# FFN projections of a macaron decoder trunk: three 256-column matmuls per weight tile in place of a 512- and a 256-column one, at other start addresses

## The chip, the cores and the metric

The kernel runs on one core of a Trainium2 chip. The metric is device time of one execution in microseconds (us); lower is better. Engines are named as the profile names them: PE is the tensor engine's matmul, PEld its weight load, DVE the vector engine, ACT the scalar engine, POOL GpSimd, SP the engine that issues most DMAs.

## What is computed

The reference is a decoder trunk with two layers on a sequence of 256 positions, D_MODEL = 1024, D_FF = 2816, all in float32. Cut to what matters:

```python
for layer in range(DEPTH):
    x = x + 0.5 * swiglu_ffn(rms_norm(x, ffn1_norm[layer]), ffn1_w_gate_up[layer], ffn1_w_down[layer])
    h = rms_norm(x, mix_norm[layer])
    x = x + (conv_mixers(h, ...) if layer % 2 == 0 else dilated_attention(h, ...))
    x = x + 0.5 * swiglu_ffn(rms_norm(x, ffn2_norm[layer]), ffn2_w_gate_up[layer], ffn2_w_down[layer])
return rms_norm(x, final_norm)

def swiglu_ffn(x, w_gate_up, w_down):
    gate, up = jnp.split(x @ w_gate_up, 2, axis=-1)
    return (jax.nn.silu(gate) * up) @ w_down
```

So there are four FFNs, with a convolution mixer after the first and attention after the third.

## The kernel before

**Layout.** Activations lie transposed: `x` is 8 blocks of 128 channels by 256 positions. All weights come as one stream of 162 units of 16 tiles (128 x 128 each, 1 MB a unit), loaded on SP into `raw`.

**Products from split operands.** Float32 accuracy comes from splitting each operand into a part rounded to fp32r and its remainder. `split` (L118) turns a unit into `w1` (ACT copy, L127) and `w2` (DVE subtraction, L128); `split_to` (L184) does the same for activations, so that `xs[:, k, 0]` and `xs[:, k, 1]` (and `gs[:, f, 0]`, `gs[:, f, 1]`) are the two parts of a block, each of 256 columns, one behind the other. A product is w1·b0 + w1·b1 + w2·b0. It is written in two ways. `mm3` (L159) makes three matmuls of 256 columns into one sum (L163, L164, L165). `mm2` (L167) makes one matmul of 512 columns, w1 with both parts side by side (L169), and one of 256 columns, w2 with the first part (L170); this leaves two sums, that have to be added later. Each matmul has its own weight load. Columns that are streamed are 768 per weight tile in both.

**An FFN** (`ffn`, L365) has 22 gate/up units p, each with 16 weight tiles: 8 contraction blocks for the gate, then 8 for the up part. Most units use `project2` (L325), with a PSUM bank each for gate and up, and then `join` (L335): an ACT copy of one half of the bank (L339), a DVE addition (L340), and a multiplication by the norm's factor (L341). The first four units of the first FFN, the first two of the fourth, and the last of each (`ONES`, `ONE_END`) use `project` (L315) with `mm3`, and only the multiplication (L382). In the first FFN the first unit comes from a separate bank, computed ahead. Then follow silu, product and split into `gs` (L386 to L389). The down projection runs over 8 output blocks d of 22 tiles each; the first seven use `mm2` and two additions into `x` (L405), the last `mm3` and one. After each block, `after.add(d)` prepares the next stage's `xs` block.

**Order.** `advance` (L131) issues loads and splits a fixed number of units ahead of use. PE runs in program order. At an FFN's start the sum of squares of `x` goes through two matmuls of 256 columns (L252, L253, in `rsqrt_wide`), which are placed among the first units' matmuls.

**Start addresses.** `xs` lies in one buffer that begins at a multiple of 1024 bytes (`LINE`, `BASE`), and each norm places its `xs` at `XS_START` bytes in it: 288 or 32 for the FFNs, 192 for conv (layer 0), 256 for attention. Blocks are 2048 bytes, so every part has its start at the same place modulo 1024. `gs` is placed by `GS_START`.

**The conv mixer** uses `project`, so `mm3`, for eight of its ten column pairs, with `xs` at 192; the pairs 2 and 9 are plain float32 (L161). Attention's query and key projections use `project2` for 8 units.

Of the kernel before, what the change touches and what calls it, by code (L numbers as in the profile page):

```python
# [10 lines left out]
F32 = mybir.dt.float32  # L11
# [3 lines left out]
ALU = mybir.AluOpType  # L15
PSUM = bass.MemoryType.PSUM

P = 128
D = 1024
S = 256  # L20
DEPTH = 2
FF = 2816
ND = D // P
NF = FF // P
# [9 lines left out]
UT = 16  # L34
# [14 lines left out]
FINE = {13: 4, 14: 4, 6: 4}  # L49
PRIO_C = 500  # L50
PRIO_R = 500
ONES = [4, 0, 0, 2]
ONE_END = 1
PRIO_F = 0
FFN_STEP = 40
QK2 = 1
# [3 lines left out]
WIDEC = 0  # L60
LINE = 1024
BASE = 16512
XS_START = {"F1": (288, 32), "MX": (192, 256), "F2": (288, 32)}
GS_START = (800, 800, 800, 736)
GROUPS = ((0, 2), (2, 4), (4, 6), (6, 8))
M_POOL = [0, 0, 0, 0]
T_POOL = [0, 0, 0, 0]
# [27 lines left out]
def trunk(ctx: ExitStack, tc: tile.TileContext, xin, wst, cst, bia, idn, out):  # L95
    nc = tc.nc
# [7 lines left out]
    psb = ctx.enter_context(tc.tile_pool(name="psb", bufs=4, space=PSUM))  # L104
# [26 lines left out]
    def advance(u, ahead_split=ahead_split):  # L131
        while at["load"] < min(n_units, u + ahead_load):
            load(at["load"])
            at["load"] += 1
        while at["split"] < min(n_units, u + ahead_split):
            split(at["split"])
            at["split"] += 1
# [16 lines left out]
    def take(n):  # L154
        st = Stream(used[0])
        used[0] += n
        return st

    def mm3(o, a, b, start, stop, check=False):  # L159
        if len(a) == 1:  # L160
            nc.tensor.matmul(o, a[0], b[-1], start=start, stop=stop, skip_group_check=check)  # L161
            return
        nc.tensor.matmul(o, a[0], b[0], start=start, stop=False, skip_group_check=check)  # L163
        nc.tensor.matmul(o, a[0], b[1], start=False, stop=False, skip_group_check=check)  # L164
        nc.tensor.matmul(o, a[1], b[0], start=False, stop=stop, skip_group_check=check)  # L165

    def mm2(o, w, b, start, stop):  # L167

        nc.tensor.matmul(o, w[0], b, start=start, stop=False, skip_group_check=True)  # L169
        nc.tensor.matmul(o[:, 0], w[1], b[:, 0], start=False, stop=stop, skip_group_check=True)  # L170


    x = keep.tile([P, ND, S], F32, name="x")
# [10 lines left out]
    def split_to(o1, o2, src, scale=None):  # L184

        if scale is None:
            nc.scalar.copy(o1, src)
            nc.vector.tensor_sub(o2, src, o1.bitcast(F32))
        else:
            nc.scalar.activation(o1, src, AF.Copy, scale=scale)  # L190
            nc.vector.scalar_tensor_tensor(o2, src, scale, o1.bitcast(F32),  # L191
                                           op0=ALU.mult, op1=ALU.subtract)
# [119 lines left out]
    def twice(r):  # L312
        return r[:, None, :].to_broadcast([P, 2, S])

    def project(st, base, xs, xg=None):  # L315

        bank = psa.tile([P, 2, S], F32, name="pa")
        for i in range(2):
            for k in range(ND):
                w = st.tile(base + 2 * k + i)  # L320
                b = (xs[:, k, 0], xs[:, k, 1]) if len(w) == 2 else (xg[:, k],)
                mm3(bank[:, i], w, b, k == 0, k == ND - 1)
        return bank

    def project2(st, base, xs):  # L325

        banks = []
        for i in range(2):
            bank = psa.tile([P, 2, S], F32, name="pa")
            for k in range(ND):  # L330
                mm2(bank, st.tile(base + 2 * k + i), xs[:, k], k == 0, k == ND - 1)
            banks.append(bank)
        return banks

    def join(v, banks, r):  # L335

        for i, bank in enumerate(banks):
            h = tmp.tile([P, S], F32, name="sq")
            nc.scalar.copy(h, bank[:, 1])  # L339
            nc.vector.tensor_add(v[:, i], bank[:, 0], h)  # L340
        nc.vector.tensor_mul(v, v, twice(r))  # L341

    def ffn_first(norm, after):

        with tc.tile_pool(name="sp", bufs=1, reuse_waits="tile") as sp:
            xg = sp.tile([P, ND, S], F32, name="xg0")
            bank = psa.tile([P, 2, S], F32, name="pa")
            for k in range(ND):
                nc.vector.tensor_scalar_mul(xg[:, k], x[:, k],
                                            const[:, norm.col + k:norm.col + k + 1])  # L350
                for i in range(2):
                    c = slice((2 * k + i) * P, (2 * k + i + 1) * P)
                    nc.tensor.matmul(bank[:, i], raw[0][:, c], xg[:, k],
                                     start=k == 0 and i == 0, stop=k == ND - 1,
                                     skip_group_check=True)
            load(1)
            at["load"] = 2
            nc.sync.dma_start(ident, idn)
            at["split"] = 1
            advance(0, 2)  # L360
            for d in range(ND):
                norm.add(d)
            ffn(norm, after, first=bank)

    def ffn(norm, after, between=None, first=None):  # L365
        _, r = norm.end(True, first is None)
        with tc.tile_pool(name="gp", bufs=1, reuse_waits="tile") as gp:
            st = take(NF)
            start = GS_START[st.u // FFN_STEP] // 4
            gs = gp.tile([P, NF * 2 * S + start], F32R, name="gs")[:, start:].rearrange(  # L370
                "p (f t s) -> p f t s", f=NF, t=2)
            for p in range(NF):
                advance(st.u + p)
                one = p < ONES[st.u // FFN_STEP] or p >= NF - ONE_END
                if one:
                    bank = first if first and p == 0 else project(st, p * UT, norm.xs)
                else:
                    banks = project2(st, p * UT, norm.xs)
                with tc.high_priority(offset=PRIO_F):
                    v = tmp.tile([P, 2, S], F32, name="v")  # L380
                    if one:
                        nc.vector.tensor_mul(v, bank, twice(r))  # L382
                    else:
                        join(v, banks, r)
                    sl = tmp.tile([P, S], F32, name="sl")
                    nc.scalar.activation(sl, v[:, 0], AF.Silu)  # L386
                    g = tmp.tile([P, S], F32, name="g")
                    nc.vector.tensor_mul(g, sl, v[:, 1])
                    split_to(gs[:, p, 0], gs[:, p, 1], g)  # L389
            if between:  # L390
                between(gs[:, NF - 1, 0, :1].bitcast(F32))
            st = take(NF * ND // UT)
            for d in range(ND):
                acc = psb.tile([P, 2, S], F32, name="pb")
                two = d < ND - 1
                for f in range(NF):
                    t = d * NF + f
                    if t % UT == 0 or f == 0:
                        advance(st.u + t // UT)
                    if two:  # L400
                        mm2(acc, st.tile(t), gs[:, f], f == 0, f == NF - 1)
                    else:
                        mm3(acc[:, 0], st.tile(t), (gs[:, f, 0], gs[:, f, 1]), f == 0, f == NF - 1)
                for i in range(2 if two else 1):
                    nc.vector.scalar_tensor_tensor(x[:, d], acc[:, i], 0.5, x[:, d],  # L405
                                                   op0=ALU.mult, op1=ALU.add)
                after.add(d)

    def out_half(st, accs, half, o, ds, ahead=(ahead_split,) * 2):
# [306 lines left out]
    for _ in range(WARM):  # L716
        nc.tensor.matmul(cold, ones, ones, start=True, stop=True)
    norm = Norm(C_F1, start=XS_START["F1"][0])
    for layer in range(DEPTH):
        nxt = Norm(C_MX + layer * ND, start=XS_START["MX"][layer])  # L720
        if layer == 0:
            ffn_first(norm, nxt)
        else:
            ffn(norm, nxt)
        norm, nxt = nxt, Norm(C_F2 + layer * ND, start=XS_START["F2"][layer])
        (conv if layer % 2 == 0 else attention)(norm, nxt)
        if layer < DEPTH - 1:
            norm, nxt = nxt, Norm(C_F1 + (layer + 1) * ND, start=XS_START["F1"][layer + 1])
            ffn(norm, nxt)
            norm = nxt  # L730
    with tc.tile_pool(name="fp", bufs=1, reuse_waits="tile") as fp:
# [6 lines left out]
        _, r = rsqrt_of([last.sums, last.sq], D, RMS_EPS, eps)  # L738
# [95 lines left out]
```

## Time and profile before

| | |
|---|---|
| median of 3 runs | 961.24 us (961.21 to 961.92) |
| profiled execution, its own time | 960.91 us |
| its span, first to last instruction | 958.8 us |
| outside the span | 2.1 us |
| PE busy | 944.7 us, 99% |
| DVE busy | 731.8 us, 76% |
| ACT busy | 548.9 us, 57% |
| POOL busy | 47.9 us, 5% |
| mean DMA rate | 184 GB/s |

The profile is one execution taken by the hardware profiler. A group row gives line, engine, operation, result and operands, shape and count, then busy time, mean duration of one, and idle time before it with what ended it. Matmuls are pipelined, one begins before the one ahead has ended, so the sum of their durations is more than the time they take; the pace is read from start to start, in the timeline. A timeline row gives the start in us from the span's start, the duration in us, and the instruction.

### The profile page before, as it was taken

How to read it: one execution, taken by the hardware profiler on the slowest of the kernel's cores; microseconds unless marked ns; L12 is line 12 of the kernel's file. 1: busy time of each engine (PE TensorE's matmuls, PEld its weight loads, DVE VectorE, ACT ScalarE, POOL GpSimd, SP SyncE). 2: the span in 40 equal slices, each digit the busy share in tenths (PEclk: the TensorE clock that was granted, in tenths of full speed). 3: DMA queues.
4: the chain of work that ended last, by engine and by line, in shares of the span. 5: the costliest groups of instructions: out<-in, count | busy, mean ns of one | idle time of the engine just before them, and what ended most of it. 6: DMA issues, size and time to landing. Idle time of an engine off the chain costs nothing.

```text
span 958.8 us, 15184 instructions
## 1 busy us (share of the span) xinstructions
PE 944.7 (99%) x5860; PEld 847.1 (88%) x5860; DVE 731.8 (76%) x1383; ACT 548.9 (57%) x985; POOL 47.9 (5%) x61
## 2 busy tenths in 40 slices
PE   9999999999899999999999999999999999999996
PEld 8988898999798888988988889898888998889886
DVE  8988776688999888766788877665698798787552
ACT  6665654497366665544466565444666565665540
POOL 0000000049600000000000000000000000000000
PEclk9999999999999999999999999999999999999998
DMA  9865565543175555555455555556553455555501
GB/s 337 290 213 177 184 212 176 191 161 133 45 284 186 203 204 176 187 209 176 176 201 195 178 197 197 179 201 212 187 198 123 157 184 189 200 194 179 200 17 44
DMA packets 27288, 176.26 MB, mean 184 GB/s; under 512 B 3024, under 2 KB 3792, under 8 KB 6864
## 3 DMA queue, kind: packets, MB, share of 16 engines
q1 hardware_dynamic: 26784, 174.67, 52.2%
q8 instruction: 46, 0.75, 0.3%
q10 hardware_dynamic: 432, 0.63, 0.2%
q14 instruction: 26, 0.21, 0.1%
HBM read 174.23 MB, written 1.05 MB: 183 GB/s over the span
## 4 chain that ended last, share of the span: by engine, by line
PE 91%; DVE 3%; ACT 2%; POOL 1%; issue 1%; DMA 0%; SPq 0%; DVEq 0%; POOLq 0%; ACTq 0%
PE pa L169 33%; PE pa L170 17%; PE pb L169 15%; PE pb L170 8%; PE pa L163 4%; PE pa L164 4%; PE pa L165 4%; PE pa L161 2%; ACT prod L486 1%; DVE pb L464 1%; PE pb L163 1%; PE pb L164 1%; PE pb L165 1%; POOL yp L487 1%; DVE w L128 1%
## 5 line engine op out<-in xcount | busy, mean ns | idle before, releaser
L128 DVE TENSOR_TENSOR w<-raw,w 128x1024 fp32r<-128x1024 f32 (+1 forms) x322 | 381.5, 1196 | 133.6 <-ACT w L127 133.0
L169 PE MATMUL pa<-xs,w 128*128 128x512 f32 x1376 | 479.1, 391 | 0.0
L127 ACT CAST w<-raw 128x1024 fp32r<-128x1024 f32 (+1 forms) x322 | 325.0, 1027 | 134.3 <-PE pa L169 50.0
L170 PE MATMUL pa<-xs,w 128*128 128x256 f32 x1376 | 387.6, 282 | 0.0
L169 PEld LDWEIGHTS pa<-xs,w 128*128 128x128 f32 x1376 | 258.3, 188 | 54.8 <-DVE xs L191 0.5
L170 PEld LDWEIGHTS pa<-xs,w 128*128 128x128 f32 x1376 | 260.0, 189 | 0.1
L169 PE MATMUL pb<-gs,w 128*128 128x512 f32 x616 | 213.7, 390 | 0.0
L170 PE MATMUL pb<-gs,w 128*128 128x256 f32 x616 | 173.7, 282 | 0.0
L169 PEld LDWEIGHTS pb<-gs,w 128*128 128x128 f32 x616 | 115.6, 188 | 24.1
L170 PEld LDWEIGHTS pb<-gs,w 128*128 128x128 f32 x616 | 116.4, 189 | 0.0
L386 ACT ACTIVATE sl<-v 128x256 f32<-128x256 f32 x88 | 36.8, 418 | 106.0 <-DVE v L341 102.0
L339 ACT COPY sq<-pa 128x256 f32<-128x256 f32 x172 | 63.3, 368 | 30.1 <-PE pa L170 24.9
L164 PE MATMUL pa<-xs,w 128*128 128x256 f32 x272 | 76.2, 281 | 0.1
L163 PE MATMUL pa<-xs,w 128*128 128x256 f32 x272 | 76.2, 282 | 0.0
L165 PE MATMUL pa<-xs,w 128*128 128x256 f32 x272 | 76.1, 280 | 0.0
L340 DVE TENSOR_TENSOR v<-pa,sq 128x256 f32<-128x256 f32 x156 | 65.1, 418 | 0.0
L405 DVE SCALAR_TENSOR_TENSOR x<-pb,x 128x256 f32<-128x256 f32 x60 | 25.4, 423 | 42.5 <-PE pb L170 28.5
L487 POOL TENSOR_TENSOR yp<-yp,prod 128x256 f32<-128x256 f32 x55 | 46.3, 845 | 207.8 <-ACT prod L486 203.8
L190 ACT ACTIVATE xs<-x,const 128x256 fp32r<-128x256 f32 x48 | 24.2, 506 | 54.8 <-DVE x L405 43.0
L341 DVE TENSOR_TENSOR v<-v,rr 128x512 f32<-128x512 f32 x78 | 53.4, 684 | 0.0
L164 PEld LDWEIGHTS pa<-xs,w 128*128 128x128 f32 x272 | 51.5, 189 | 0.5 <-DVE xs L191 0.3
L165 PEld LDWEIGHTS pa<-xs,w 128*128 128x128 f32 x272 | 51.1, 188 | 0.2 <-DVE w L128 0.2
(160 smaller groups left out, 926.5 us busy)
## 6 DMA issues: line engine op xcount, KB each, us to landing
raw<-wst SPq DMA_DIRECT2D x159, 1024.0 KB, 4.8
bt<-bia SPq DMA_DIRECT2D x8, 384.0 KB, 3.6
raw<-wst SPq DMA_DIRECT2D x7, 256.0 KB, 6.0
raw<-wst SPq DMA_DIRECT2D x2, 512.0 KB, 6.0
x<-xin SPq DMA_DIRECT2D x3, 256.0 KB, 4.9
out<-y SPq DMA_DIRECT2D x2, 256.0 KB, 2.5
out<-y ACTq DMA_DIRECT2D x2, 256.0 KB, 2.4
x<-xin SPq DMA_DIRECT2D x2, 128.0 KB, 3.1
```

The lines of the kernel that those rows point to most:

```text
L127: nc.scalar.copy(w1[u][:, c], raw[u][:, c])
L128: nc.vector.tensor_sub(w2[u][:, c], raw[u][:, c], w1[u][:, c].bitcast(F32))
L163: nc.tensor.matmul(o, a[0], b[0], start=start, stop=False, skip_group_check=check)
L164: nc.tensor.matmul(o, a[0], b[1], start=False, stop=False, skip_group_check=check)
L165: nc.tensor.matmul(o, a[1], b[0], start=False, stop=stop, skip_group_check=check)
L169: nc.tensor.matmul(o, w[0], b, start=start, stop=False, skip_group_check=True)
L170: nc.tensor.matmul(o[:, 0], w[1], b[:, 0], start=False, stop=stop, skip_group_check=True)
L339: nc.scalar.copy(h, bank[:, 1])
L340: nc.vector.tensor_add(v[:, i], bank[:, 0], h)
L341: nc.vector.tensor_mul(v, v, twice(r))
L386: nc.scalar.activation(sl, v[:, 0], AF.Silu)
L487: nc.gpsimd.tensor_add(yp[:, c], yp[:, c], t)
```

## The change

All FFN units use `project` and all output blocks `mm3`. `ONES` and `ONE_END`, and with them `project2` and `join` in the FFNs, go; the second addition at L405 goes, and `acc` is 256 columns wide. The FFNs' `xs` start at 192 instead of 288 or 32, and `gs` at 960 or 896 instead of 800 or 736. With 960 the gated products are 192 bytes past a multiple of 1024; with 800, which is 160 less, they were 32 bytes past one. Attention keeps `project2` and its start of 256, conv its start of 192.

```diff
-ONES = [4, 0, 0, 2]
-ONE_END = 1
...
-XS_START = {"F1": (288, 32), "MX": (192, 256), "F2": (288, 32)}
-GS_START = (800, 800, 800, 736)
+XS_START = {"F1": (192, 192), "MX": (192, 256), "F2": (192, 192)}
+GS_START = (960, 960, 960, 896)
...
             for p in range(NF):
                 advance(st.u + p)
-                one = p < ONES[st.u // FFN_STEP] or p >= NF - ONE_END
-                if one:
-                    bank = first if first and p == 0 else project(st, p * UT, norm.xs)
-                else:
-                    banks = project2(st, p * UT, norm.xs)
+                bank = first if first and p == 0 else project(st, p * UT, norm.xs)
                 with tc.high_priority(offset=PRIO_F):
                     v = tmp.tile([P, 2, S], F32, name="v")
-                    if one:
-                        nc.vector.tensor_mul(v, bank, twice(r))
-                    else:
-                        join(v, banks, r)
+                    nc.vector.tensor_mul(v, bank, twice(r))
...
             for d in range(ND):
-                acc = psb.tile([P, 2, S], F32, name="pb")
-                two = d < ND - 1
+                acc = psb.tile([P, S], F32, name="pb")
                 for f in range(NF):
                     t = d * NF + f
                     if t % UT == 0 or f == 0:
                         advance(st.u + t // UT)
-                    if two:
-                        mm2(acc, st.tile(t), gs[:, f], f == 0, f == NF - 1)
-                    else:
-                        mm3(acc[:, 0], st.tile(t), (gs[:, f, 0], gs[:, f, 1]), f == 0, f == NF - 1)
-                for i in range(2 if two else 1):
-                    nc.vector.scalar_tensor_tensor(x[:, d], acc[:, i], 0.5, x[:, d],
-                                                   op0=ALU.mult, op1=ALU.add)
+                    mm3(acc, st.tile(t), (gs[:, f, 0], gs[:, f, 1]), f == 0, f == NF - 1)
+                nc.vector.scalar_tensor_tensor(x[:, d], acc, 0.5, x[:, d],
+                                               op0=ALU.mult, op1=ALU.add)
                 after.add(d)
```

## Rows read from the trace of the kernel before

**Rows 1.** the page: busy time, granted clock by slice, chain by engine
```profile
PE 944.7 (99%) x5860; PEld 847.1 (88%) x5860; DVE 731.8 (76%) x1383; ACT 548.9 (57%) x985; POOL 47.9 (5%) x61
...
PEclk9999999999999999999999999999999999999998
...
PE 91%; DVE 3%; ACT 2%; POOL 1%; issue 1%; DMA 0%; SPq 0%; DVEq 0%; POOLq 0%; ACTq 0%
```

**Rows 2.** waits of PE: who waited for whom, us in total, times, longest
```profile
PE pa L161 <- DVE ya L539: 3.8, 1, 3.8
```

**Rows 3.** groups by line and form, matmuls: xcount | busy us, mean ns
```profile
L169 PE MATMUL pa<-xs,w 128*128 128x512 f32 x1376 | 479.1, 391 | 0.0
...
L169 PE MATMUL pb<-gs,w 128*128 128x512 f32 x616 | 213.7, 390 | 0.0
...
L163 PE MATMUL pa<-xs,w 128*128 128x256 f32 x272 | 76.2, 282 | 0.0
...
L163 PE MATMUL pb<-gs,w 128*128 128x256 f32 x88 | 24.5, 279 | 0.0
```

**Rows 4.** the same view, copies and elementwise work after the matmuls
```profile
L339 ACT COPY sq<-pa 128x256 f32<-128x256 f32 x172 | 63.3, 368 | 30.1 <-PE pa L170 24.9 <-DVE v L340 3.7 <-DVE sq L188 1.1
...
L340 DVE TENSOR_TENSOR v<-pa,sq 128x256 f32<-128x256 f32 x156 | 65.1, 418 | 0.0
...
L341 DVE TENSOR_TENSOR v<-v,rr 128x512 f32<-128x512 f32 x78 | 53.4, 684 | 0.0
...
L382 DVE TENSOR_TENSOR v<-pa,rr 128x512 f32<-128x512 f32 x10 | 6.9, 686 | 0.4
...
L405 DVE SCALAR_TENSOR_TENSOR x<-pb,x 128x256 f32<-128x256 f32 x60 | 25.4, 423 | 42.5 <-PE pb L170 28.5 <-PE pb L165 12.7
```

**Rows 5.** PE timeline, first down projection: start us, us, instruction
```profile
130.31 0.39 PE L169 MATMUL pb<-gs,w 128*128 128x512 f32 x1
...
183.70 0.28 PE L163 MATMUL pb<-gs,w 128*128 128x256 f32 x1
```

**Rows 6.** PE timeline, last gate/up unit of the same FFN
```profile
124.71 0.28 PE L163 MATMUL pa<-xs,w 128*128 128x256 f32 x1
...
130.19 0.28 PE L165 MATMUL pa<-xs,w 128*128 128x256 f32 x1
```

**Rows 7.** PE timeline, conv projection, second pair
```profile
198.90 0.28 PE L164 MATMUL pa<-xs,w 128*128 128x256 f32 x1
...
204.23 0.59 PE L161 MATMUL pa<-xg,raw 128*128 128x256 f32 x2
```

**Rows 8.** PE timeline, conv projection, fourth to ninth pair
```profile
211.25 0.28 PE L164 MATMUL pa<-xs,w 128*128 128x256 f32 x1
...
245.06 0.60 PE L161 MATMUL pa<-xg,raw 128*128 128x256 f32 x2
```

**Rows 9.** PE timeline, conv projection, first pair
```profile
191.75 0.28 PE L163 MATMUL pa<-xs,w 128*128 128x256 f32 x1
...
193.68 0.28 PE L165 MATMUL pa<-xs,w 128*128 128x256 f32 x1
...
194.28 0.39 PE L164 MATMUL pa<-xs,w 128*128 128x256 f32 x1
...
195.34 0.28 PE L164 MATMUL pa<-xs,w 128*128 128x256 f32 x1
...
197.34 0.28 PE L163 MATMUL pa<-xs,w 128*128 128x256 f32 x1
```

**Rows 10.** PE timeline, third FFN, where the sum of squares comes in
```profile
471.48 0.36 PE L252 MATMUL pb<-sq,ones 128*128 128x256 f32 x1
471.67 0.39 PE L169 MATMUL pa<-xs,w 128*128 128x512 f32 x1
```

**Rows 11.** PE timeline, output projection of conv, reading ob
```profile
281.84 0.28 PE L165 MATMUL pa<-ob,w 128*128 128x256 f32 x1
...
282.56 0.28 PE L165 MATMUL pa<-ob,w 128*128 128x256 f32 x1
```

## The prediction

> **What bounds the kernel now.** I read the page first. PE is busy 99% of the span at the full granted clock in nearly every slice, and it holds 91% of the chain that ended last [rows 1]. Then the waits of PE: the first and longest of seven is 3.8 us, in the conv mixer [rows 2], and no line of an FFN's projections is among them. So the FFNs are bound by how fast PE gets through its own stream, and the change is judged by one number, the time PE takes for one weight tile, times the number of tiles. How many tiles there are comes from the groups [rows 3]; the pace comes from the timeline, start to start, since durations overlap.
>
> **The pace of both forms.** In the first down projection 154 tiles of the two-matmul form lie between the start at 130.31 and that at 183.70: 53.39 / 154 = 346.7 ns a tile [rows 5]. The last gate/up unit just ahead of it runs the three-matmul form at today's FFN address: 48 matmuls from 124.71 to the 130.31 of rows 5, 116.7 ns each, 350.0 ns a tile [rows 5, 6]. At the address that the change moves everything to, 192, only the conv mixer runs mm3, and there the trace shows two paces for the same line, the same operands and the same address. The second pair takes 5.33 us for 47 starts, 113.4 ns each, 340.2 ns a tile [rows 7]. The fourth to ninth pairs take 33.81 us for 287 starts, 117.8 ns each, 353.4 ns a tile [rows 8]. Each, once it is there, holds to the end of its stretch. This is the disputed price, and it lies on both sides of 346.7.
>
> **The change part by part.** *Matmuls.* L169 has 1376 pairs in `pa`; 78 joined units of 16 tiles are FFN work (156 additions at L340, two a unit [rows 4]), so 1248, and the other 128 are attention's and stay. In `pb` there are 616 [rows 3]. So 1864 tiles change form, and 1864 matmuls and weight loads are added, all on PE's path. The FFN tiles that are already mm3 change only their address: 272 at L163 in `pa` less conv's eight pairs of 16, so 144, and 88 in `pb` [rows 3]: 232.
>
> The bounds: at 340.2 the sum is 1864 x (-6.5) + 232 x (-9.8) = -12.1 - 2.3 = -14.4 us. At 353.4 it is 1864 x 6.7 + 232 x 3.4 = 12.5 + 0.8 = +13.3 us. Beyond the upper end lies what mm3 shows from `ob`: six starts in 0.72 us, 120 ns, 360 ns a tile [rows 11], worth 1864 x 13.3 + 232 x 10 = +27 us; I use it only as an outlying case.
>
> I take 353.4, because of how each pace was entered. In conv's first pair the stream ran on from the down projection without a break and went at 1.93 us for 17 starts, 113.5 ns; then three starts took 0.60 us instead of 0.34, up to 194.28, the norm's small matmuls followed, and the stream came back at 2.00 us for 17 starts, 117.6 ns [rows 9]. After pair 2, which is another kind of matmul, it came back at 117.8 again and stayed for 34 us [rows 8]. Against this, the second pair followed on the norm's transposing matmuls and ran fast [rows 7]. So of three returns after a break two are slow and one is fast. Each FFN begins with such a break: the sum of squares' matmul, 0.19 us before the next start instead of about 0.12 [rows 10]. After it nothing in an FFN breaks the stream, gate/up and down have one address in the new kernel, and the pace that it falls into should hold for the FFN's 524 tiles on average. Each FFN is a draw of its own, worth (13.3 + 14.4) / 4 = 6.9 us between its two outcomes.
>
> [...]
>
> *Joins.* 156 ACT copies of 368 ns (L339) and 156 DVE additions of 418 ns (L340) go, 57 and 65 us; 78 multiplications from SBUF (684 ns, L341) become 78 from PSUM (686 ns, L382) [rows 4]. *Output blocks.* 28 of 60 additions at L405 go, 12 us of DVE [rows 4]. All this lies beside PE's stream and covers nothing on its path, so I cost it at 0, between 0 and -1 us: the small stops at the FFNs' starts (as the 0.07 us at L252) are all it could shorten, and each FFN's last unit and last block have the short form already. If the cover goes, that is if PE becomes so fast that ACT or DVE is late, there is ample room: DVE at 76% loses 77 us of work.
>
> *Loads and splits.* `advance` issues the same units in the same order; nothing is moved past a queue, no wait is added, and PSUM needs one bank a unit instead of two. 0 us; the shorter ACT queue can only bring splits earlier.
>
> **The sum.** 1864 x 6.7 + 232 x 3.4 = +13.3 us on the profiled execution's own 960.91 (span 958.8 and 2.1 around it): 974.2. The median of the runs is 0.3 us above that execution, so 974.5 us.
>
> **The rivals.** *Fast in all FFNs* (the other sign): the stream enters each FFN in step, as conv's first pair did [rows 9], and keeps 340.2. It decides at the first matmuls behind the sum of squares. For it: the fast pace held over a change of bank and weights for 5 us [rows 7], and in the new kernel down and next gate/up have the same address. Against it: the breaks. 961.2 - 14.4 = 946.8 us. With three FFNs fast and one slow it is 953.7, with two and two 960.7.
>
> *The address plays no part*: mm3 goes at the 350.0 that the FFNs show, 1864 x 3.3 = +6.2, 967.4 us. For it: 350.0 is what this form does in this very stage. Against it: 113.4, 117.8 and 120 ns for one line at three places [rows 7, 8, 11]. The Trainium skill ("SBUF — State Buffer", section "Who interferes with whom") gives PE two independent read ports and says that it waits on no one, by which an address would not matter; the three paces disagree. Three slow FFNs and one fast give nearly the same time, 967.6.
>
> *The change doesn't do what it says*: the joins' 134 us on ACT and DVE bring time back. The waits leave no place for it; at most 1 us, inside the ranges.
>
> **How the numbers follow.** About 0.2% is what a measurement of this kernel can tell from no change, 1.9 us. All four slow 0.35 (974.5); three slow 0.12 (967.6); 350 throughout 0.09 (967.4); two and two 0.09 (960.7, of which 0.04 same, 0.03 faster, 0.02 slower); three fast 0.11 (953.7); all fast 0.22 (946.8); 360 throughout 0.02 (988). Slower: 0.35 + 0.12 + 0.09 + 0.02 + 0.02 = 0.60. Faster: 0.22 + 0.11 + 0.03 = 0.36. Same 0.04. To leave out all four fast would leave out more than 2 in 10, so the range reaches from 946.0 (946.8 and up to 1 us of freed waits) to 976.0; the likeliest case alone has 972.5 to 976.
>
> **What would show it.** A unit of 48 matmuls in an FFN should take 5.65 us from start to start in the timeline; 5.44 is the fast rival, 5.60 the one without address, against 5.55 for today's two-matmul form. ACT should lose 57 us and DVE 77, with no change of PE's waits. The prediction is wrong if the FFNs' mm3 settles at 113 ns after the sum of squares, or if the pace changes in mid-stage.

## The result, and the profile after

The changed kernel takes 975.32 us (median of 4 runs, 970.69 to 976.58) against 961.47 us before: ratio 1.0131, 95% interval 1.0117 to 1.0144. The forecast was 974.5 us, slower. The profiled execution took 974.77 us, with a span of 973.0 us.

From the page of the changed kernel: busy time, granted clock by slice, and the chain by engine.

```profile
PE 957.0 (98%) x7724; PEld 933.2 (96%) x7724; DVE 668.6 (69%) x1199; ACT 499.0 (51%) x829; POOL 47.9 (5%) x61
...
PEclk9999999999999999999999999999999999999998
...
PE 92%; DVE 3%; ACT 2%; POOL 1%; DMA 1%; issue 0%; SPq 0%; DVEq 0%; POOLq 0%; ACTq 0%
```

Against [rows 1]: 1864 matmuls and as many weight loads more, as counted, at the same clock. PE is still the chain. DVE and ACT have less to do, which bought nothing, as `e2` below shows.

The groups by line and form (the lines have moved up: L161 to L163 are the three matmuls, L337 the copy in a join, L375 the multiplication from PSUM, L391 the addition into `x`):

```profile
L161 PE MATMUL pa<-xs,w 128*128 128x256 f32 x1520 | 426.6, 281 | 0.0
...
L161 PE MATMUL pb<-gs,w 128*128 128x256 f32 x704 | 197.8, 281 | 0.0
...
L375 DVE TENSOR_TENSOR v<-pa,rr 128x512 f32<-128x512 f32 x88 | 60.9, 692 | 116.5 <-PE pa L163 116.4
...
L391 DVE SCALAR_TENSOR_TENSOR x<-pb,x 128x256 f32<-128x256 f32 x32 | 13.5, 423 | 45.5 <-PE pb L163 45.5
...
L337 ACT COPY sq<-pa 128x256 f32<-128x256 f32 x16 | 5.8, 363 | 1.5 <-PE pa L168 1.5
```

Of the joins of [rows 4] only attention's 16 copies are left, and 28 additions at L391 are gone.

The PE timeline, first and second down projection, from the first matmul to the one after the last:

```profile
133.22 0.28 PE L161 MATMUL pb<-gs,w 128*128 128x256 f32 x1
...
195.41 0.28 PE L161 MATMUL pa<-xs,w 128*128 128x256 f32 x1
...
413.23 0.28 PE L161 MATMUL pb<-gs,w 128*128 128x256 f32 x1
...
475.41 0.28 PE L161 MATMUL pa<-xs,w 128*128 128x256 f32 x1
```

528 starts in 62.19 and 62.18 us: 117.8 ns each, 353.4 ns a tile. That is the pace of [rows 8], against 346.7 ns in [rows 5] and 116.7 ns a matmul in [rows 6]. The third and fourth FFN, and all gate/up stages behind the sum of squares, go at the same 117.8.

The waits of PE in the changed kernel, us in total, times, longest:

```profile
PE pa L159 <- DVE ya L525: 3.7, 1, 3.7
PE pa L351 <- DVE xg L347: 2.2, 1, 2.2
```

The first is that of [rows 2]. The second is the very first unit, which waits for the input; it was 0.5 us in the execution before. It varies without any change to this unit: in `e3` below, which keeps this unit as the changed kernel has it, it is 0.7 us.

### The profile page after: what moved, and what is told of

Read it like the earlier page. It is cut to its first block, busy times and chain, and to the rows that moved or that the text cites. A ratio compares the mean times of both kernels' runs of the same rounds, so it can differ in the third digit from the quotient of the medians.

```text
span 973.0 us, 18536 instructions
## 1 busy us (share of the span) xinstructions
PE 957.0 (98%) x7724; PEld 933.2 (96%) x7724; DVE 668.6 (69%) x1199; ACT 499.0 (51%) x829; POOL 47.9 (5%) x61
## 4 chain that ended last, share of the span: by engine, by line
PE 92%; DVE 3%; ACT 2%; POOL 1%; DMA 1%; issue 0%; SPq 0%; DVEq 0%; POOLq 0%; ACTq 0%
PE pa L161 19%; PE pa L162 19%; PE pa L163 19%; PE pb L163 9%; PE pb L161 9%; PE pb L162 9%; PE pa L167 3%; PE pa L159 2%; PE pa L168 2%; ACT prod L472 1%; DVE pb L450 1%; POOL yp L473 1%; PE pb L646 1%; PE pa L351 1%; DVE w L126 1%; DMA x<-xin 1%
## 5 line engine op out<-in xcount | busy, mean ns | idle before, releaser
L125 ACT CAST w<-raw 128x1024 fp32r<-128x1024 f32 (+1 forms) x322 | 323.1, 1024 | 292.5 <-PE pa L162 197.8
L162 PE MATMUL pa<-xs,w 128*128 128x256 f32 x1520 | 427.2, 281 | 0.0
L163 PE MATMUL pa<-xs,w 128*128 128x256 f32 x1520 | 426.9, 281 | 0.0
L161 PE MATMUL pa<-xs,w 128*128 128x256 f32 x1520 | 426.6, 281 | 0.0
L162 PEld LDWEIGHTS pa<-xs,w 128*128 128x128 f32 x1520 | 288.6, 190 | 0.6 <-DVE xs L189 0.4
L163 PEld LDWEIGHTS pa<-xs,w 128*128 128x128 f32 x1520 | 286.8, 189 | 0.4 <-DVE w L126 0.4
L161 PEld LDWEIGHTS pa<-xs,w 128*128 128x128 f32 x1520 | 286.5, 189 | 0.3
L163 PE MATMUL pb<-gs,w 128*128 128x256 f32 x704 | 197.8, 281 | 0.0
L161 PE MATMUL pb<-gs,w 128*128 128x256 f32 x704 | 197.8, 281 | 0.0
L162 PE MATMUL pb<-gs,w 128*128 128x256 f32 x704 | 197.8, 281 | 0.0
L375 DVE TENSOR_TENSOR v<-pa,rr 128x512 f32<-128x512 f32 x88 | 60.9, 692 | 116.5 <-PE pa L163 116.4
L162 PEld LDWEIGHTS pb<-gs,w 128*128 128x128 f32 x704 | 133.7, 190 | 0.0
L161 PEld LDWEIGHTS pb<-gs,w 128*128 128x128 f32 x704 | 132.9, 189 | 0.0
L163 PEld LDWEIGHTS pb<-gs,w 128*128 128x128 f32 x704 | 132.9, 189 | 0.0
L185 ACT CAST gs<-g 128x256 fp32r<-128x256 f32 x88 | 35.7, 407 | 33.9 <-DVE g L379 33.5
L167 PE MATMUL pa<-xs,w 128*128 128x512 f32 x128 | 45.7, 400 | 0.0
L391 DVE SCALAR_TENSOR_TENSOR x<-pb,x 128x256 f32<-128x256 f32 x32 | 13.5, 423 | 45.5 <-PE pb L163 45.5
L186 DVE TENSOR_TENSOR gs<-g,gs 128x256 fp32r<-128x256 f32 x88 | 36.9, 421 | 0.0
```

Of the source, the lines that this page charges most:

```text
L125: nc.scalar.copy(w1[u][:, c], raw[u][:, c])
```

## The experiments

**Theory:** PE's pace in an FFN is set by the start address of the streamed operand; at 192 three matmuls have two paces, and what ran just ahead in the stream decides which. **Rivals:** the third matmul and weight load cost the time, whatever the address; or 192 is always slow in an FFN. Times are medians, ratios are to the kernel before on the same chip.

### Form and address, one at a time

`e1_three_at_32`, the changed kernel at the old addresses:

```diff
-XS_START = {"F1": (192, 192), "MX": (192, 256), "F2": (192, 192)}
-GS_START = (960, 960, 960, 896)
+XS_START = {"F1": (288, 32), "MX": (192, 256), "F2": (288, 32)}
+GS_START = (800, 800, 800, 736)
```

> The changed kernel with the old start addresses (inputs at 288 or 32, gated products at 32). Theory (the pace of three matmuls depends on the start address, and at 32 it is the 116.7 ns that the few such units of the kernel before showed): 116.7 ns from start to start in all four FFNs, 350 ns a tile, 1864 x 3.3 ns = +6.2 us, about 967.6 us against 961.5. Rival (the third matmul and weight load cost the time, the address plays no part): 117.8 ns and about 975 us as in the changed kernel.

Measured: 969.15 us, ratio 1.0077 (1.0058 to 1.0096). Its first down projection in the timeline:

```profile
132.24 0.28 PE L161 MATMUL pb<-gs,w 128*128 128x256 f32 x1
...
193.84 0.28 PE L161 MATMUL pa<-xs,w 128*128 128x256 f32 x1
```

528 starts in 61.60 us, 116.7 ns. The pace is the theory's to the digit; the time is 1.5 us over the expected 967.6. The kernel before, too, took 0.7 us more on this chip (962.15 us) than the 961.5 that the expectation started from. In the profiled execution about 1 us lies in the start-up: its first down projection begins 1.9 us later than in [rows 5], where 17 units x 16 tiles x 3.3 ns explain 0.9.

`e2_two_at_192`, the kernel before at the new addresses, the same edit the other way round in the kernel before.

> The kernel before with the new start addresses (192) and its two matmuls. Theory (the address sets the pace of either form, by an interplay of the streamed read with the next weight load): the tile no longer takes 346.7 ns; by how much is open, between 340 ns (-12 us) and 353 ns (+12 us). Rival (the address matters to nothing, only the number of matmuls): 346.7 ns a tile and 961.5 us.

Measured: 974.15 us, ratio 1.013 (1.0115 to 1.0145). The first down projection, up to its first matmul of the three-matmul form:

```profile
132.58 0.40 PE L169 MATMUL pb<-gs,w 128*128 128x512 f32 x1
...
186.99 0.28 PE L163 MATMUL pb<-gs,w 128*128 128x256 f32 x1
```

154 tiles in 54.41 us: 353.3 ns, where [rows 5] had 346.7. Not one instruction differs from the kernel before, only where the operands lie, and the whole loss is there. With joins or without, with two matmuls a tile or three, the pace at 192 is the same (353.3 and 353.4 ns a tile), and so is the time: 974.15 and 975.32 us. So the joins' removal bought nothing, and at this address, in the slow pace, the third matmul cost nothing either.

### Other addresses

`o0` and `o64` are the changed kernel with other starts:

```diff
# o0
-XS_START = {"F1": (192, 192), "MX": (192, 256), "F2": (192, 192)}
-GS_START = (960, 960, 960, 896)
+XS_START = {"F1": (256, 256), "MX": (192, 256), "F2": (256, 256)}
+GS_START = (768, 768, 768, 704)
# o64
+XS_START = {"F1": (64, 64), "MX": (192, 256), "F2": (64, 64)}
+GS_START = (832, 832, 832, 768)
```

> The changed kernel with inputs at 256 and gated products at a multiple of 256, the place where the conv mixer's ob lay when its line showed 120 ns in the kernel before. Theory (the start address sets the pace): 120 ns in all FFNs, 2096 tiles x 360 ns against 346.7 or 350: +27 us, about 988 us. Rival (ob's 120 ns came from the mixer's other work, and address only matters between odd places): 117.8 ns, 975 us.

> The changed kernel with inputs and gated products 64 bytes past a multiple of 1024 instead of 192. If only the place modulo 128 counts, it is like 192: 117.8 ns in some FFNs or all (113.4 in others), 947 to 975 us. If each start address has its own pace, something else, between 113 and 120 ns.

Measured, one run each: `o0` 990.79 us, `o64` 977.77 us. Their first down projections, `o0` first:

```profile
137.71 0.28 PE L161 MATMUL pb<-gs,w 128*128 128x256 f32 x1
...
201.07 0.29 PE L161 MATMUL pa<-xs,w 128*128 128x256 f32 x1
```

```profile
135.70 0.28 PE L161 MATMUL pb<-gs,w 128*128 128x256 f32 x1
...
197.88 0.28 PE L161 MATMUL pa<-xs,w 128*128 128x256 f32 x1
```

63.36 and 62.18 us for 528 starts: 120.0 and 117.8 ns. So the 120 ns of `ob` [rows 11] goes with its place. The 2.5 us by which `o64` is slower than the changed kernel, at the same pace, lie ahead of the first down projection, which begins at 135.70 instead of 133.22 us. 64 gave the slow pace of 192 in all four FFNs, which fits a rule of 128 bytes and doesn't prove it: 96, 128 and 160 were not run, nor was a second pace looked for at 64.

### The entry

`e3_three_32_then_192` is the changed kernel with the inputs back at 288 and 32, so that of the FFNs only down is at 192:

```diff
-XS_START = {"F1": (192, 192), "MX": (192, 256), "F2": (192, 192)}
+XS_START = {"F1": (288, 32), "MX": (192, 256), "F2": (288, 32)}
```

> The changed kernel with inputs at 288 or 32 and gated products at 192, so that each down projection is entered without a break from a stream at 116.7 ns, as the conv mixer's first pair was in the kernel before. Theory (at 192 two paces are possible, and the entry decides which): gate/up at 116.7 ns (+4.1 us), down at 113.4 ns (616 x -6.5 and 88 x -9.8 ns = -4.9 us), together about 960.7 us. Rival (117.8 ns is what 192 gives in an FFN, whatever the entry): down at 117.8 ns, +4.4 us, about 970 us.

Measured: 963.28 us over ten runs (961.49 to 964.31), ratio 1.0011 (1.0001 to 1.002), between the two expectations. The timeline, first and second down projection:

```profile
132.68 0.28 PE L161 MATMUL pb<-gs,w 128*128 128x256 f32 x1
...
192.54 0.28 PE L161 MATMUL pa<-xs,w 128*128 128x256 f32 x1
...
409.17 0.28 PE L161 MATMUL pb<-gs,w 128*128 128x256 f32 x1
...
471.36 0.28 PE L161 MATMUL pa<-xs,w 128*128 128x256 f32 x1
```

59.86 us (113.4 ns) in the first and 62.19 us (117.8 ns) in the second, in one execution, for the same line and address; the third and fourth were like the first. So both paces exist in an FFN, and an unbroken entry from 32 gave the fast one in three of four, not in all.

`e4_two_up_three_down` keeps the two-matmul form and its joins in gate/up, and takes three matmuls at 192 in down:

```diff
-GS_START = (800, 800, 800, 736)
+GS_START = (960, 960, 960, 896)
...
-                two = d < ND - 1
+                two = False
```

> The kernel before (two matmuls at 288 or 32 in gate/up, with its joins) with three matmuls throughout in down and gated products at 192. Each down projection is entered without a break from the last gate/up unit, which is of the three-matmul form at 32. Theory (entry decides): down at 113.4 ns, 616 x -6.5 and 88 x -9.8 ns = -4.9 us, about 956.6 us, faster than both kernels. Rival (192 is slow in an FFN): down at 117.8 ns, +4.4 us, about 965.9 us.

Measured: 956.67 us, ratio 0.9946 (0.9931 to 0.9961), as the theory has it and faster than both kernels. Its timeline, first down projection:

```profile
131.33 0.28 PE L163 MATMUL pb<-gs,w 128*128 128x256 f32 x1
...
191.18 0.28 PE L163 MATMUL pa<-xs,w 128*128 128x256 f32 x1
```

And its group of down matmuls, by line and form (busy us, mean ns):

```profile
L163 PE MATMUL pb<-gs,w 128*128 128x256 f32 x704 | 194.4, 276 | 0.0
```

59.85 us, 113.4 ns, and a mean of 276 ns over all four FFNs where the changed kernel has 281.

### Setting the entry by hand

`k1_nine_at_32` puts nine matmuls, whose sum nobody reads, ahead of the fourth unit of each FFN of the changed kernel. `k2_nine_at_192` is the control, `k3_three_at_32` has three, `k4_one_at_32` one, `k6_three_earlier` has three a unit earlier in three of the FFNs.

```diff
+KICK_AT = 3
+KICKS = 9
+KICK = (1024 + 32) // 4
...
                 advance(st.u + p)
+                if p == KICK_AT:
+                    spare = psb.tile([P, S], F32, name="pb")
+                    for i in range(KICKS):
+                        nc.tensor.matmul(spare, st.tile(p * UT)[0], xs_all[:, KICK:KICK + S],
+                                         start=i == 0, stop=i == KICKS - 1)
# k2: KICK = (1024 + 192) // 4; k3: KICKS = 3; k4: KICKS = 1; k6: KICKS = 3, KICK_AT = (2, 2, 2, 3)
```

> The changed kernel, and at the fourth unit of each FFN nine matmuls more, of the same form, into a spare bank that nobody reads, with their streamed operand at 32 past a multiple of 1024 instead of 192. They leave the computation as it is and cost 9 x 0.117 = 1.1 us an FFN, 4.2 us in all. Theory (at 192 there are two paces, and an unbroken stream at 32 ahead of it lets it into the fast one): from there on gate/up and down at 113.4 ns, 1920 tiles x 13.2 ns = -25.3 us, together about 954 us. Rival (the two paces belong to something else in those stages, as conv's small matmuls or down's blocks): 117.8 ns throughout and 979.5 us.

> The control for the run with nine matmuls at 32: the same nine into the same spare bank, but with the streamed operand at 192 like all others. Theory (it is the jump of address that changes the pace): 117.8 ns stays, 975.3 + 4.2 = 979.5 us. Rival (any nine matmuls, or the change of bank and accumulation, shift the stream): 113.4 ns and about 954 us.

Measured: `k1` 956.37 us (953.53 to 957.23), ratio 0.9932 (0.9915 to 0.9949); `k2` 980.45 us (972.77 to 982.11), ratio 1.0171 (1.0121 to 1.022). First FFN of `k1`, from the first matmul behind the sum of squares, by the nine, to the end of gate/up:

```profile
16.38 0.28 PE L164 MATMUL pa<-xs,w 128*128 128x256 f32 x1
...
25.92 1.22 PE L378 MATMUL pb<-xs,w 128*128 128x256 f32 x9
26.97 0.28 PE L164 MATMUL pa<-xs,w 128*128 128x256 f32 x1
...
130.34 0.28 PE L164 MATMUL pb<-gs,w 128*128 128x256 f32 x1
```

The same places in `k2`:

```profile
16.42 0.28 PE L164 MATMUL pa<-xs,w 128*128 128x256 f32 x1
...
25.96 1.22 PE L378 MATMUL pb<-xs,w 128*128 128x256 f32 x9
27.02 0.28 PE L164 MATMUL pa<-xs,w 128*128 128x256 f32 x1
...
134.44 0.28 PE L164 MATMUL pb<-gs,w 128*128 128x256 f32 x1
```

Ahead of the nine both go at 117.8 ns (81 starts in 9.54 us). Behind them 912 starts (19 units of 48) take 103.37 us, 113.3 ns, with the nine at 32, and 107.42 us, 117.8 ns, with the nine at 192. Instruction for instruction the two kernels are alike; only the address of nine unread matmuls differs, and the pace of the 912 that follow, and of the down projection behind them, goes with it in all four FFNs of the two traces. In `k1` three of the four turned from slow to fast at the nine; its third FFN was at 113 ns already. In `k2` all four were slow ahead of the nine and stayed so. This settles that the address of a few matmuls in the stream can switch the pace. One of `k2`'s four runs took 972.77 us, about 7 us less than the profiled one, which one fast FFN would explain; it has no trace.

> As the run with nine matmuls at 32, with three. Theory (one jump of address in an unbroken stream is enough): 113.4 ns behind them in all four FFNs, 6 matmuls fewer an FFN, 24 x 0.117 = 2.8 us less than with nine, about 953.5 us by the medians. Rival (the stream must first settle into the pace of 32, which takes more than three): 117.8 ns stays in some or all FFNs, up to 976.7 us.

> As the run with nine matmuls at 32, with a single one. Theory (one jump is enough): 113.4 ns in all four FFNs, 3.7 us less than with nine, about 952.6 us. Rival (it must settle at 32 first): 117.8 ns stays in some or all, up to 975.8 us.

Measured: `k3` 951.84 us (950.72 to 953.84), ratio 0.9896 (0.9879 to 0.9912). That is 1.7 us under the expected 953.5, less than the 3.7 us between `k1`'s own four runs, from whose median the 953.5 was reckoned. Behind its three matmuls every FFN of its profile is fast. Its second FFN, from behind the sum of squares:

```profile
290.36 0.28 PE L164 MATMUL pa<-xs,w 128*128 128x256 f32 x1
...
299.78 0.52 PE L378 MATMUL pb<-xs,w 128*128 128x256 f32 x3
300.13 0.28 PE L164 MATMUL pa<-xs,w 128*128 128x256 f32 x1
...
403.51 0.28 PE L164 MATMUL pb<-gs,w 128*128 128x256 f32 x1
```

80 starts in 9.42 us (117.8 ns) ahead of the three, 912 in 103.38 us (113.4 ns) behind them; the third and fourth FFN turn in the same way.

`k4` took 957.35 us, the median of ten runs, which reach from 949.65 to 970.18. Its profiled execution, the quickest, is fast in all four FFNs, in the first one ahead of its matmul already. One more run took 951.45 us. The rest lie from 955 to 959, at 964 and 966, and at 970, which is what one, two or three FFNs at the slow pace would add at 6.9 us each; those runs have no trace, so this is argued. One matmul is not a safe way in; three were in these runs.

> The two-matmul form at 192 (the kernel before at the new start addresses, about 974 us) with the same nine matmuls at 32 ahead of the fourth unit. Theory (the slow pace at 192 is one of two for this form as well, and the number of matmuls is of no weight there): the tile falls from 353.4 to about 340 ns, 974.2 + 4.2 - 1920 x 0.0134 = about 953 us. Rival (the second pace belongs to the three-matmul form): 353.4 ns a tile stays, about 978 us; or 346.7, about 965 us.

`k5_two_nine_at_32` has the same nine in `e2`. Measured: 977.69 us, ratio 1.0165 (1.0148 to 1.0182): the rival. First down projection up to the first matmul of the other form:

```profile
133.96 0.40 PE L172 MATMUL pb<-gs,w 128*128 128x512 f32 x1
...
188.37 0.28 PE L166 MATMUL pb<-gs,w 128*128 128x256 f32 x1
```

154 tiles in 54.41 us, 353.3 ns still. The nine did their work here, too, as long as three matmuls followed. The fourth unit of the first FFN still has the three-matmul form in this kernel; its first matmul behind the nine, and the first one of the two-matmul form:

```profile
26.76 0.28 PE L166 MATMUL pa<-xs,w 128*128 128x256 f32 x1
...
32.21 0.39 PE L172 MATMUL pa<-xs,w 128*128 128x512 f32 x1
```

48 starts in 5.45 us, 113.5 ns; then the two-matmul form goes at 353 ns a tile. So the fast pace at 192 was not to be had with two matmuls, not even straight out of it; there the form does matter.

> The run with three matmuls at 32, with the three a unit earlier in the first three FFNs, still behind both matmuls of the sum of squares. Theory (from the jump on, until something breaks the stream, the pace is 113.4 ns): 3 units x 16 tiles x 13.2 ns = 0.6 us less than with the three at the fourth unit, about 951.2 us, and fast behind them in all four FFNs. Rival (the place matters, for instance because a wait still follows in those units): 117.8 ns in one FFN or more, 958 us and above.

Measured: 951.23 us (951.03 to 952.29), ratio 0.989 (0.9873 to 0.9906), the lowest median here. The 0.6 us to `k3` is the one expected, but the runs of the two overlap, so it isn't shown. All four FFNs of the profiled execution are fast behind the three, the first one ahead of them already.

## Why the prediction was right

**The bound and the term.** PE's own stream bounds the FFNs, before and after, and the change was worth 1864 x 6.7 + 232 x 3.4 ns = +13.3 us. The profiled executions differ by 974.77 - 960.91 = 13.9 us; about 0.9 us of it is start-up, where the first matmuls waited 2.2 us for the input instead of 0.5. (That wait is of an FFN's projection after all, though the prediction found none among PE's waits.) The pace taken from conv [rows 8], 353.4 ns a tile, was met in each of the four FFNs.

**The choice between two paces.** This was the weak step: three returns after a break, two of them slow. It came out as taken, and `k1` against `k2` show half of its ground to be sound: what the stream held just before can decide the pace at 192. The other half, that the break sets the pace and that it then holds, failed in the changed kernel's own trace. Its third FFN, around the sum of squares (L250 is its first matmul, with the break behind it, L251 its second):

```profile
479.10 0.35 PE L250 MATMUL pb<-sq,ones 128*128 128x256 f32 x1
...
479.41 0.28 PE L163 MATMUL pa<-xs,w 128*128 128x256 f32 x1
...
480.09 0.28 PE L163 MATMUL pa<-xs,w 128*128 128x256 f32 x1
480.21 0.28 PE L251 MATMUL pb<-sq,ones 128*128 128x256 f32 x1
480.32 0.28 PE L161 MATMUL pa<-xs,w 128*128 128x256 f32 x1
...
481.97 0.28 PE L161 MATMUL pa<-xs,w 128*128 128x256 f32 x1
```

Behind the break the stream is fast, 6 starts in 0.68 us (113 ns). Behind the second matmul, which comes without a break, it is slow: 14 starts in 1.65 us (118 ns), and so to the FFN's end. Six traces enter the FFNs with all starts at 192, the changed kernel and `k1` to `k4` and `k6` ahead of their spare matmuls. In their second to fourth FFNs PE reached the second matmul at the fast pace in 8 of 18 cases, and behind it was slow in 17 of 18. The prediction reckoned with the first matmul alone. Why the pace turns there was not tested.

So the price and the slow pace came out right, but the reason given for it fails in that FFN, and that all four came out slow was in part luck. The first FFN still looks like a draw, fast in three of the six traces (`k3`, `k4`, `k6`), and only two of the six have four slow entries, about the 0.35 of the prediction. One of the four runs of the changed kernel took 970.69 us, which a fast stretch would explain. The conv mixer's fourth to ninth pairs, at 192 in every run, show a draw as well: 117.8 ns in eleven of the fourteen traces, 113.3 in `k2`, `k3` and `k6`.

**The joins at 0.** Right. Their removal took 156 x 368 ns off ACT and 156 x 418 ns off DVE, and `e2`, which keeps them, is not slower than the changed kernel. The page's busy time fell by less than the forecast 57 and 77 us, by 49.9 on ACT and 63.2 on DVE: the forecast added up durations, and the page counts the time of overlapping instructions once.

**What the prediction had in the wrong place.** It spoke of tiles that "change form", as if the third matmul carried the loss. `e2` shows that the addresses alone cost +12.0 us with the old form (974.15 against 962.15), and `e1` that the form alone costs about +7 us at 32. The two do not add up: at 192, in the slow pace, the forms are equal, and only with three matmuls did a faster pace show. The rival by which the address plays no part fell with `e1`, `e2` and `o0`. The fast rival had its price right, too: `e4`, with down alone at the fast pace, took 956.67 us where -4.9 us puts 956.6, and `k3`, with some units still slow, lies 10 us below the kernel before.

The Trainium skill ("SBUF — State Buffer", section "Who interferes with whom") says that PE never waits on anyone. `e2` has a tile at 353.3 ns instead of 346.7 by address alone, for which that rule has no place; whether PE waits there for another reader is not shown.

**What stays open.** That the streamed read and the next matmul's weight load meet in the memory is a guess; no run separated the two. Nor is it shown why 32 mostly leads into the fast pace, why it did not in the second FFN of `e3`, and how long either would last if broken.

## What to carry to other kernels

When a kernel is bound by back-to-back matmuls, read their pace from start to start, and look for the same line at two paces before pricing a change of form: here the three-matmul form took from 951.2 (`k6`) to 990.8 us (`o0`) by what addresses the stream held, while the form alone was worth about 7 us at 32 and nothing at 192 in the slow pace. Change address and form apart, and try a few starts: of those tried here only 192 showed the fast pace. Where two paces occur at one address, a few spare matmuls of another address in the stream may set the better one (here 12 matmuls took the changed kernel from 975.3 to 951.8 us, 10 us below the kernel before), but look at every stage of the trace, and at the spread of the runs, before counting on it.

## What the runs showed of the hardware that was not expected

- Three fp32r matmuls of 256 columns, each with its weight load, follow at 113.3, 116.7, 117.8 or 120.0 ns at the same granted clock (1.00 in these stretches), by the start of the streamed operand modulo 1024 bytes: 120.0 at 0 modulo 256, 116.7 at 32, 117.8 at 64, and 113.3 or 117.8 at 192.
- At 192 either pace holds for some 1400 matmuls without a change (gate/up and down of one FFN), and three unread matmuls at 32 turned the slow into the fast one (`k3`). The pace also turned the other way at a single matmul, the second one of the sum of squares: 113 ns ahead of it, 118 behind it, in the changed kernel's third FFN.
- One 512- and one 256-column matmul take 346.7 ns together at 32 and 353.3 at 192, and no second pace appeared there even behind the nine at 32.
- The duration that a row gives for a matmul is no measure of the pace across addresses: at 117.8 ns it is 281 ns at 192, and in `o64` less, as its group shows:

```profile
L161 PE MATMUL pb<-gs,w 128*128 128x256 f32 x704 | 196.6, 279 | 0.0
```
